# One factor for two query blocks in a differential attention on one Trainium2 core

## The chip, the core and the metric

The kernel runs on one core of a Trainium2 chip. A core has five engines with a queue each: TensorE (PE, matmuls and transposes, into PSUM), VectorE (DVE), ScalarE (ACT, exponentials and copies), GpSimd (POOL) and SyncE (SP, which here issues the DMAs). An engine takes its instructions strictly in the order of its queue; between engines, semaphores hold an instruction back until what it reads is there and what it overwrites has been read. The metric is the device time of one execution in microseconds (us). Before the change the median of three executions is 1089.66 us (1088.95 to 1091.61).

## The reference

One layer of a hybrid decoder, sequence 1024, width 1024, all in float32: a norm, one input projection, four mixers side by side (pooling, short convolution, a Conformer convolution, differential attention), an output projection, and a gated feed-forward part of width 2816. The change is in the attention: 4 heads, each with two softmaxes over 32-wide queries and keys, values 64 wide.

```python
def block(args):                      # 8 query blocks of 128 rows
    qblk, start = args
    ...
    sc = jnp.einsum('bqhmd,bkhmd->bhmqk', qblk, k).astype(jnp.float32) * scale + bias
    sc = jnp.where(dist >= 0, sc, NEG_INF)
    p = jax.nn.softmax(sc, axis=-1)
    a = p[:, :, 0] - lam * p[:, :, 1]
    return jnp.einsum('bhqk,bkhd->bqhd', a.astype(v.dtype), v)
...
o = rms_norm(o, subln_g) * (1.0 - lam_init)
```

## The kernel before

The program has three parts: norm and input projection with the convolutions (to about 255 us), attention with the output projection filled in between (about 255 to 430 us), and the feed-forward part. A float32 matmul is made of three matmuls of high and low parts (lines 138 to 140, and 599 to 601 for the filler).

Attention works in 16 units: `for u in range(16)` with p = 0 to 3 (a pair of query blocks, i = 0 and 1, so that keys up to w = 128 x (2p + 1 + i) count) and head h = 0 to 3 inside. In a unit, for each block i and for each softmax m = 1, then 0:

- line 668: TensorE makes the scores `sc` (queries QT by keys KT). For p = 0 and 1 both softmaxes of a block share one PSUM tile (`both`), for p = 2 and 3 each has its own; there are two such tiles in turn.
- lines 675 and 676: VectorE takes the minimum over the columns (`fmx`, then `mx` with the bias table `tb` added in place; the scores are negated). 675 is there from p = 1 on.
- line 679: ScalarE writes the exponentials `pt` and their row sums into `lt`. The tile `pt` of m = 1 has two buffers (PT1), that of m = 0 has four (PT0).
- lines 681 to 683: VectorE makes the factor `cf` = l0 * (-lam) / l1, in a reciprocal and a one-column multiplication, and combines `pt0 + cf * pt1` in place. The row is not divided by l0; the norm behind it makes up for this.

Then, for each pair of key blocks: line 694 transposes the combined tile on TensorE (`tp`), line 698 copies it on ScalarE and line 699 subtracts on VectorE for the low part (`at`), and line 703 multiplies by the values (`av`). Every second head ends with a transposition of the output (715), every fourth with its norm (725 to 734). `prep_q` (lines 500 to 508) prepares the queries of the next pair in between.

What sets the order: each engine's queue is made when the program is built, by a scheduler that goes by the order of the code as priority and by its own model of times and buffers. The filler matmuls of the output projection are handed out by a fixed list of counts (FQ) at marked places, each behind a given TensorE instruction. So where an instruction stands in a queue does not change at run time. DMAs are issued by SyncE; none belongs to the lines of the change.

Of the kernel before, what the change touches and what calls it, by code (L numbers as in the profile page):

```python
# [11 lines left out]
F = mybir.dt.float32  # L12
R = mybir.dt.float32r
AF = mybir.ActivationFunctionType
ALU = mybir.AluOpType
# [4 lines left out]
P = 128  # L20
# [46 lines left out]
def tile_hybrid(ctx, tc, x, norm1_g, w_in, pool_w, pool_scale, sconv_w, conf_w, conf_b, ln_g, ln_b,  # L67
# [3 lines left out]
    V, A, G, T = nc.vector, nc.scalar, nc.gpsimd, nc.tensor  # L71
# [11 lines left out]
    def pool(name, bufs=1, side="left", **kw):  # L83
        return tc.tile_pool(name=name, bufs=bufs, side=side, reuse_waits="tile", **kw)
# [4 lines left out]
    sm = ctx.enter_context(pool("sm"))  # L89
# [28 lines left out]
    def cp(e, dst, src):  # L118
        if e == 0:
            A.copy(dst, src)  # L120
        else:
            (V, G)[e - 1].tensor_copy(dst, src)
# [119 lines left out]
    for p in range(4):  # L242
# [13 lines left out]
        h = p // 2  # L256
# [80 lines left out]
    nlam = const.tile([P, 1], F, name="nlam")  # L337
# [242 lines left out]
    def ps_sc():  # L580
        return pss.tile([P, 1024], F, name="sc", tag="sc")

    def ps_tp():
        return psp.tile([P, 512], F, name="tp", tag="tp")

    def ps_av():
        return psq.tile([P, 512], F, name="av", tag="av")
# [48 lines left out]
    def fill1(ins, n=None):  # L636
        for _ in range(next(slots, 0) if n is None else n):
            while fillq:
                f = next(fillq[0], None)
                if f is not None:  # L640
                    if GATE:
                        with tc.issue_after(ins.ins):
                            f()
                    else:
                        f()
                    break
                fillq.pop(0)
# [4 lines left out]
    def unit(u, p, h):  # L652
        if h == 0:
            pend["lt"] = sm.tile([P, 4, 2, 2], F, name="lt", tag="lt", bufs=2)
            pend["o"] = sm.tile([P, 2, 4, 64], F, name="o", tag="kn")
        lt, o = pend["lt"], pend["o"]
        Ps = []
        for i in range(2):
            w = P * (2 * p + 1 + i)
            nw = min(w, 256)  # L660
            pts = [None, None]
            both = ps_sc() if p < 2 else None
            for m in MO:
                hm = 2 * h + m
                sc = ps_sc() if both is None else both[:, 512 * m:512 * m + 512]
                for c0 in range(0, w, 512):
                    n = min(max(w - c0, 256), 512)
                    ins = T.matmul(sc[:, c0:c0 + n], lhsT=QT[p, h // 2][:, hm % 4, i * P:(i + 1) * P],
                                   rhs=KT[h // 2][:, hm % 4, c0:c0 + n], start=True, stop=True)
                fill1(ins)  # L670
                mx = sm.tile([P, 1], F, name="mx", tag="mx", bufs=4)
                init = 3.0e38
                if w > 256:
                    init = sm.tile([P, 1], F, name="fmx", tag="fmx", bufs=2)
                    V.tensor_reduce(init, sc[:, 0:w - 256], axis=AX.X, op=ALU.min)
                V.tensor_tensor_reduce(out=sc[:, w - nw:w], in0=sc[:, w - nw:w], in1=tb[:, h, 256 - nw:], scale=1.0,  # L676
                                       scalar=init, op0=ALU.add, op1=ALU.min, accum_out=mx)
                pts[m] = ap4.tile([P, S], F, name="pt", tag=f"pt{m}", bufs=PT1 if m else PT0)
                A.activation(pts[m][:, 0:w], sc[:, 0:w], AF.Exp, bias=mx, scale=-1.0, accum_out=lt[:, h, m, i:i + 1])  # L679
            cf = sm.tile([P, 1], F, name="cf", tag="cf", bufs=4)  # L680
            V.reciprocal(cf, lt[:, h, 1, i:i + 1])
            V.scalar_tensor_tensor(cf, lt[:, h, 0, i:i + 1], nlam, cf, op0=ALU.mult, op1=ALU.mult)
            V.scalar_tensor_tensor(pts[0][:, 0:w], pts[1][:, 0:w], cf, pts[0][:, 0:w], op0=ALU.mult, op1=ALU.add)  # L683
            Ps.append(pts[0])
        if h % 2 == 0:
            pend["av"] = ps_av()
        avs = pend["av"]
        av = avs[:, (h % 2) * 256:(h % 2) * 256 + 256]
        for kb in range(p + 1):
            ps = ps_tp()  # L690
            blocks = [(a, i) for a in range(2) for i in range(2) if 2 * kb + a <= 2 * p + i]
            nb = len(blocks) * P
            for j, (a, i) in enumerate(blocks):
                ins = T.transpose(ps[:, j * P:(j + 1) * P], Ps[i][:, (2 * kb + a) * P:(2 * kb + a + 1) * P], ident)
            marks.append(ins)
            fill1(ins)
            at = ap4.tile([P, 2, 512], R, name="at", tag="at", bufs=ATB)
            A.copy(at[:, 0, 0:nb], ps[:, 0:nb])
            V.tensor_tensor(at[:, 1, 0:nb], ps[:, 0:nb], at[:, 0, 0:nb].bitcast(F), op=ALU.subtract)
            for s in range(2):  # L700
                for a in range(2):
                    n = min(nb - 256 * a, 256)
                    ins = T.matmul(av[:, 256 - n:256], lhsT=VV[kb][:, a, h, :], rhs=at[:, s, 256 * a:256 * a + n],
                                   start=(kb == 0 and a == 0 and s == 0), stop=(kb == p and a == 1 and s == 1))
                if s == 0:
                    fill1(ins)
        marks.append(ins)
        fill1(ins)
        if h % 2 == 1:
            oT = sm.tile([P, 512], F, name="oT", tag="sq")  # L710
            cp(OTE[u // 2], oT, avs)
            ps = ps_tp()
            for hh in range(2):
                for i in range(2):
                    ins = T.transpose(ps[:, (i * 2 + hh) * P:(i * 2 + hh + 1) * P], oT[:, hh * 256 + i * P:hh * 256 + (i + 1) * P], ident)
            marks.append(ins)
            fill1(ins)
            psv = ps.rearrange("p (i h d) -> p i h d", i=2, h=2)
            ov = o[:, :, h - 1:h + 1, :]
            cp(OVE[u // 2], ov, psv[:, :, :, 64:128])  # L720
            V.tensor_tensor(ov, ov, psv[:, :, :, 0:64], op=ALU.add)
        if h == 3:
            of = o.rearrange("p i h d -> p (i h) d")
            osq = sm.tile([P, 8, 64], F, name="osq", tag="sq")
            A.activation(osq, of, AF.Square)
            rr = sm.tile([P, 2, 4], F, name="rr", tag="rr", bufs=2)
            rrf = rr.rearrange("p i h -> p (i h)")
            V.tensor_reduce(rrf, osq, axis=AX.X, op=ALU.add)
            l0 = lt[:, :, 0, :]
            l2 = sm.tile([P, 4, 2], F, name="l2", tag="l2", bufs=2)  # L730
            V.scalar_tensor_tensor(l2, l0, EPS, l0, op0=ALU.mult, op1=ALU.mult)
            V.scalar_tensor_tensor(rr, rr, 1.0 / 64, l2.rearrange("p h i -> p i h"), op0=ALU.mult, op1=ALU.add)
            G.tensor_tensor(rrf, rrf, mhalf[:, 0:8], op=ALU.pow)
            (G if X5[PO.index(p)] else V).tensor_tensor(qn[p].rearrange("p i (h d) -> p (i h) d", h=4), of, rrf.unsqueeze(2).broadcast_to([P, 8, 64]),
                            op=ALU.mult)
# [85 lines left out]
    for u in range(16):  # L821
        j, h = u // 4, u % 4
        p = PO[j]
        if h == 0 and j > 0:
            fillq.append(out_attn(PO[j - 1]))
            if j == 3:
                fillq.append(norm2(PO[0]))
                fillq.append(norm2(PO[1]))
        if h == PQ1 and j > 0:
            prep_q(p, 1, ps_tp, 4, fill1)  # L830
        if h == PQ0 and j < 3:
            prep_q(PO[j + 1], 0, ps_tp, 4, fill1)
        unit(u, p, h)
# [345 lines left out]
```

## Time and profile before

| | |
|---|---|
| median of 3 executions | 1089.66 us |
| the profiled execution | 1092.04 us |
| its span, first to last instruction | 1090.2 us |
| TensorE clock, mean granted | 0.995 |
| PE / DVE / ACT / POOL busy | 97 / 67 / 40 / 21% |

A busy share is over the whole span. In a window of time the busy times of the engines can be set against the length of the window; what is missing is idle time of that engine. Matmuls overlap each other, so that a busy TensorE is not one at its peak.

### The profile page before, as it was taken

What the parts mean: (1) busy time and instruction counts of PE and PEld (TensorE: products, weight loads), DVE (VectorE), ACT (ScalarE), POOL (GpSimd) and SP (SyncE); (2) the same over time, 40 slices, a digit from 0 to 9 for tenths busy, and PEclk for the clock granted to TensorE, in tenths of its full rate; (3) what the DMA queues carried; (4) which work ended last, traced back from release to release, by engine and by line L of the source; (5) the groups of instructions that cost most, each with busy time, mean ns of one, the idle gap of its engine ahead of it and who ended that gap; (6) DMA issues with size and microseconds to landing.
All of it is one profiled execution on the core that took longest, in us unless ns stands there. A gap on an engine that the chain in (4) does not pass through costs nothing.

```text
span 1090.2 us, 13509 instructions
## 1 busy us (share of the span) xinstructions
PE 1054.3 (97%) x5203; PEld 875.9 (80%) x5203; DVE 734.6 (67%) x1127; ACT 439.4 (40%) x710; POOL 224.1 (21%) x202
## 2 busy tenths in 40 slices
PE   7989999998989999999999999999999999999998
PEld 6858888997778876787778888888888888888886
DVE  5599965556899977788677766565556666655541
ACT  5511123544787676442333332333333244333320
POOL 5224423673757743210000000000000000000000
PEclk9989999999999999999999999999999999999999
DMA  8230111110111122013567663233223268766731
GB/s 217 45 97 25 54 39 39 40 40 30 39 50 58 40 78 58 1 58 135 201 238 267 240 242 111 73 126 108 86 97 126 72 237 295 264 193 199 234 108 39
DMA packets 89664, 128.04 MB, mean 117 GB/s; under 512 B 17112, under 2 KB 57600, under 8 KB 87040
## 3 DMA queue, kind: packets, MB, share of 16 engines
q1 hardware_dynamic: 89600, 127.18, 35.6%
q8 instruction: 41, 0.67, 0.2%
q14 instruction: 23, 0.19, 0.1%
HBM read 94.13 MB, written 33.04 MB: 117 GB/s over the span
## 4 chain that ended last, share of the span: by engine, by line
PE 78%; DVE 11%; DMA 6%; ACT 2%; issue 1%; POOL 1%; SPq 0%; ACTq 0%; POOLq 0%; DVEq 0%
PE sb L140 10%; PE sb L138 10%; PE sb L139 10%; PE mm L139 6%; PE mm L140 6%; PE mm L138 6%; PE dx L140 3%; PE dx L139 3%; PE dx L138 3%; PE dy L140 3%; PE dy L139 2%; PE dy L138 2%; DMA wd<-in_w_down_dram 2%; DMA dT<-wd 2%; DVE pt L683 1%
## 5 line engine op out<-in xcount | busy, mean ns | idle before, releaser
L138 PE MATMUL sb<-T,rhi 128*128 128x512 f32 x320 | 125.6, 393 | 0.0
L140 PE MATMUL sb<-T,rlo 128*128 128x512 f32 x320 | 125.4, 392 | 0.0
L139 PE MATMUL sb<-T,rhi 128*128 128x512 f32 x320 | 125.4, 392 | 0.0
L906 DVE TENSOR_TENSOR dq<-ds,dq 128x2048 fp32r<-128x2048 f32 x35 | 80.1, 2290 | 60.4 <-ACT dq L905 60.4
L905 ACT CAST dq<-ds 128x2048 fp32r<-128x2048 f32 x35 | 66.8, 1911 | 105.5 <-PE dy L140 40.4
L134 POOL TENSOR_TENSOR wlo<-st,whi 128x1024 fp32r<-128x1024 f32 (+2 forms) x30 | 73.3, 2447 | 111.4 <-ACT whi L120 98.1
L139 PE MATMUL mm<-hT,whi 128*128 128x512 f32 (+1 forms) x224 | 82.1, 371 | 1.0 <-DVE hT L200 1.0
L138 PE MATMUL mm<-hT,whi 128*128 128x512 f32 (+1 forms) x224 | 80.3, 374 | 1.8 <-ACT hT L199 1.8
L140 PE MATMUL mm<-hT,wlo 128*128 128x512 f32 (+1 forms) x224 | 81.5, 368 | 0.0
L312 DVE SCALAR_TENSOR_TENSOR t<-u,cw,t 128x1023 f32<-128x1023 f32 (+28 forms) x58 | 71.2, 1265 | 0.7
L138 PEld LDWEIGHTS sb<-T,rhi 128*128 128x128 f32 x320 | 60.1, 188 | 13.8 <-DVE afs L1014 0.3
L139 PEld LDWEIGHTS sb<-T,rhi 128*128 128x128 f32 x320 | 60.1, 188 | 13.5
L140 PEld LDWEIGHTS sb<-T,rlo 128*128 128x128 f32 x320 | 60.0, 188 | 13.5
L905 ACT CAST rhi<-st 128x1024 fp32r<-128x1024 f32 x28 | 29.4, 1052 | 84.6 <-PE sb L139 53.0
L140 PE MATMUL dx<-dq 128*128 128x512 f32 x160 | 62.3, 390 | 0.0
L139 PE MATMUL dx<-dq 128*128 128x512 f32 x160 | 62.2, 389 | 0.0
L138 PE MATMUL dx<-dq 128*128 128x512 f32 x160 | 61.8, 389 | 0.0
L679 ACT ACTIVATE pt<-sc,mx 128x128 f32<-128x128 f32 (+7 forms) x64 | 47.6, 747 | 18.7 <-DVE mx L676 18.6
L138 PE MATMUL mm<-whi,hT 128*128 128x256 f32 x192 | 54.8, 289 | 0.0
L139 PE MATMUL mm<-wlo,hT 128*128 128x256 f32 x192 | 54.5, 285 | 0.0
L140 PE MATMUL mm<-whi,hT 128*128 128x256 f32 x192 | 54.4, 284 | 0.0
L120 ACT CAST whi<-st 128x1024 fp32r<-128x1024 f32 x28 | 29.4, 1050 | 59.7 <-PE mm L139 53.0
(342 smaller groups left out, 2690.1 us busy)
## 6 DMA issues: line engine op xcount, KB each, us to landing
ds<-dL SPq DMA_DIRECT2D x35, 512.0 KB, 4.1
wd<-in_w_down_dram SPq DMA_DIRECT2D x10, 1024.0 KB, 5.1
dT<-wd SPq DMA_DIRECT2D x10, 1024.0 KB, 4.0
dL<-afs SPq DMA_DIRECT2D x10, 1024.0 KB, 4.1
ds<-dT SPq DMA_DIRECT2D x20, 512.0 KB, 5.3
st<-in_w_in_dram SPq DMA_DIRECT2D x18, 512.0 KB, 3.8
st<-in_w_gate_dram SPq DMA_DIRECT2D x15, 512.0 KB, 4.3
st<-in_w_up_dram SPq DMA_DIRECT2D x15, 512.0 KB, 3.7
```

The source lines that it names most:

```text
L120: A.copy(dst, src)
L134: G.tensor_tensor(lo[:, nv:], st[:, nv:], hi[:, nv:].bitcast(F), op=ALU.subtract)
L138: T.matmul(ps, lhsT=L[0], rhs=Rr[0], start=first, stop=False, skip_group_check=more)
L139: T.matmul(ps, lhsT=L[0], rhs=Rr[1], start=False, stop=False, skip_group_check=more)
L140: return T.matmul(ps, lhsT=L[1], rhs=Rr[0], start=False, stop=last, skip_group_check=more)
L312: V.scalar_tensor_tensor((z if s == 30 else acc)[:, s:], u[:, :S - s], w[:, 30 - s:31 - s], acc[:, s:], op0=ALU.mult, op1=ALU.add)
L679: A.activation(pts[m][:, 0:w], sc[:, 0:w], AF.Exp, bias=mx, scale=-1.0, accum_out=lt[:, h, m, i:i + 1])
L683: V.scalar_tensor_tensor(pts[0][:, 0:w], pts[1][:, 0:w], cf, pts[0][:, 0:w], op0=ALU.mult, op1=ALU.add)
L905: A.copy(hi, src)
L906: (eng or V).tensor_tensor(lo, src, hi.bitcast(F), op=ALU.subtract)
```

## The change

The factor is made once in a unit, for both query blocks, as two columns: one reciprocal and one multiplication. Both combinations stand behind it, so behind the exponentials of both blocks. In the changed file the lines behind line 683 are three further down: the combination is 686, the transposes 697, the subtraction 702.

```diff
-            cf = sm.tile([P, 1], F, name="cf", tag="cf", bufs=4)
-            V.reciprocal(cf, lt[:, h, 1, i:i + 1])
-            V.scalar_tensor_tensor(cf, lt[:, h, 0, i:i + 1], nlam, cf, op0=ALU.mult, op1=ALU.mult)
-            V.scalar_tensor_tensor(pts[0][:, 0:w], pts[1][:, 0:w], cf, pts[0][:, 0:w], op0=ALU.mult, op1=ALU.add)
-            Ps.append(pts[0])
+            Ps.append(pts)
+        cf = sm.tile([P, 2], F, name="cf", tag="cf", bufs=4)
+        V.reciprocal(cf, lt[:, h, 1, :])
+        V.scalar_tensor_tensor(cf, lt[:, h, 0, :], nlam, cf, op0=ALU.mult, op1=ALU.mult)
+        for i, (a, b) in enumerate(Ps):
+            w = P * (2 * p + 1 + i)
+            V.scalar_tensor_tensor(a[:, 0:w], b[:, 0:w], cf[:, i:i + 1], a[:, 0:w], op0=ALU.mult, op1=ALU.add)
+        Ps = [a for a, b in Ps]
```

The scheduler orders the engines anew from the first unit to the end of attention; SyncE's queue stays as it was, and so does everything behind attention.

VectorE from the end of unit 6 into unit 7 (p = 1). Before; `pt_3047` is the combined block 1 of unit 6, `sc_3079` and `sc_3099` are the scores of unit 7:

```order
L683 SCALAR_TENSOR_TENSOR pt_3047<-pt_3040,cf_3049,pt_3047 128x512
L721 TENSOR_TENSOR o_2779<-o_2779,tp_2969 128x2x128
L681 RECIPROCAL cf_3095<-lt_2778 128x1
L675 TENSOR_REDUCE fmx_3090<-sc_3079 128x1
L675 TENSOR_REDUCE fmx_3107<-sc_3099 128x1
L676 ISA sc_3079,mx_3089<-sc_3079,tb_783,fmx_3090 128x256
L676 ISA mx_3089 128x1
L676 ISA sc_3099,mx_3106<-sc_3099,tb_783,fmx_3107 128x256
L676 ISA mx_3106 128x1
L682 SCALAR_TENSOR_TENSOR cf_3095<-lt_2778,nlam_627,cf_3095 128x1
```

Now; `pt_3009` and `pt_3025` are the two blocks of unit 6, `sc_3058` and `sc_3074` the scores of unit 7:

```order
L683 SCALAR_TENSOR_TENSOR cf_3027<-lt_2766,nlam_627,cf_3027 128x2
L686 SCALAR_TENSOR_TENSOR pt_3009<-pt_2993,cf_3027,pt_3009 128x384
L686 SCALAR_TENSOR_TENSOR pt_3025<-pt_3018,cf_3027,pt_3025 128x512
L702 TENSOR_TENSOR at_3040<-tp_3033,at_3040 128x512
L675 TENSOR_REDUCE fmx_3069<-sc_3058 128x1
L675 TENSOR_REDUCE fmx_3082<-sc_3074 128x1
L702 TENSOR_TENSOR at_3051<-tp_3047,at_3051 128x384
L676 ISA sc_3058,mx_3068<-sc_3058,tb_783,fmx_3069 128x256
L676 ISA mx_3068 128x1
L676 ISA sc_3074,mx_3081<-sc_3074,tb_783,fmx_3082 128x256
```

The subtraction for unit 6's own transposes has come to stand ahead of the minima of unit 7.

TensorE at the same place. Before; `sc_3079` is the m = 0 score of unit 7, block 0, and `tp_3054` holds transposes of unit 6:

```order
L668 MATMUL sc_3099<-KT1_1365,QT_2750 128x512
L668 MATMUL sc_3079<-KT1_1365,QT_2750 128x384
L505 MATMUL tp_2997<-ident_89,kst_2994 128x128 x4
L600 MATMUL fm_2909<-wlo_2430,sp_2986 128x512
L601 MATMUL fm_2909<-whi_2429,sp_2986 128x512
L694 MATMUL tp_3054<-ident_89,pt_3027 128x128
L694 MATMUL tp_3054<-ident_89,pt_3047 128x128
```

Now; `sc_3058` is the m = 0 score of unit 7, block 0, and `tp_3033` and `tp_3047` hold transposes of unit 6:

```order
L697 MATMUL tp_3033<-ident_89,pt_3009 128x128
L697 MATMUL tp_3047<-ident_89,pt_3009 128x128
L697 MATMUL tp_3033<-ident_89,pt_3025 128x128
L697 MATMUL tp_3033<-ident_89,pt_3009 128x128
L697 MATMUL tp_3033<-ident_89,pt_3025 128x128
L601 MATMUL fm_3000<-whi_2417,sp_3001 128x512
L599 MATMUL fm_3000<-whi_2417,sp_3001 128x512
L697 MATMUL tp_3047<-ident_89,pt_3025 128x128 x2
L600 MATMUL fm_3000<-wlo_2418,sp_3001 128x512
L668 MATMUL sc_3058<-KT1_1365,QT_2738 128x384
```

The m = 0 score of unit 7 stood ahead of unit 6's transposes and now stands behind them.

VectorE late in unit 13 (p = 3). Before; `cf_3986` is the factor of block 1 and `sc_3977` its last scores, `sc_4070` belongs to unit 14:

```order
L676 ISA sc_3977,mx_3980<-sc_3977,tb_783,fmx_3981 128x256
L676 ISA mx_3980 128x1
L675 TENSOR_REDUCE fmx_4074<-sc_4070 128x1
L699 TENSOR_TENSOR at_3886<-tp_3879,at_3886 128x512
L676 ISA sc_4070,mx_4073<-sc_4070,tb_783,fmx_4074 128x256
L676 ISA mx_4073 128x1
L682 SCALAR_TENSOR_TENSOR cf_3986<-lt_3809,nlam_627,cf_3986 128x1
L699 TENSOR_TENSOR at_3906<-tp_3899,at_3906 128x512
L683 SCALAR_TENSOR_TENSOR pt_3984<-pt_3975,cf_3986,pt_3984 128x1024
```

Now; `cf_3943` is the one factor of unit 13, `sc_3934` the last scores, `sc_4028` belongs to unit 14:

```order
L676 ISA sc_3934,mx_3937<-sc_3934,tb_783,fmx_3938 128x256
L676 ISA mx_3937 128x1
L676 ISA sc_4028,mx_4031<-sc_4028,tb_783,fmx_4032 128x256
L676 ISA mx_4031 128x1
L702 TENSOR_TENSOR at_3867<-tp_3860,at_3867 128x512
L683 SCALAR_TENSOR_TENSOR cf_3943<-lt_3773,nlam_627,cf_3943 128x2
L686 SCALAR_TENSOR_TENSOR pt_3923<-pt_3913,cf_3943,pt_3923 128x896
L686 SCALAR_TENSOR_TENSOR pt_3941<-pt_3932,cf_3943,pt_3941 128x1024
```

Between the last minimum and the factor that needs its exponential there stand two steps now and three before, and both combinations follow.

## Rows read from the trace of the kernel before

**Rows 1.** The page, busy time, share of the span and instructions of each engine.

```profile
PE 1054.3 (97%) x5203; PEld 875.9 (80%) x5203; DVE 734.6 (67%) x1127; ACT 439.4 (40%) x710; POOL 224.1 (21%) x202
```

**Rows 2.** Stretches: length, busy PE, PEld, DVE, ACT, POOL; clock, DMA share, GB/s.

```profile
255.00:310.00 55.00, 50.27 (x264) 39.76 (x263) 47.13 (x158) 37.07 (x110) 34.66 (x40) 0.97 0.12 37
310.00:331.00 21.00, 18.35 (x109) 15.19 (x108) 20.39 (x51) 16.62 (x37) 15.10 (x13) 1.00 0.23 78
331.00:400.00 69.00, 65.95 (x379) 56.01 (x378) 64.48 (x140) 49.76 (x99) 43.98 (x43) 1.00 0.17 55
...
262.00:266.00 4.00, 3.95 (x14) 3.20 (x15) 2.62 (x11) 2.38 (x9) 0.08 (x1) 0.57 0.04 10
```

**Rows 3.** Chain that ended last, around 300 and 375 us: start, us, what.

```profile
299.92 0.53 DVE fmx L675 x2
300.45 0.40 DVE sc L676
...
302.01 0.75 DVE pt L683
...
375.20 1.47 DVE pt L683
```

**Rows 4.** Timeline, VectorE, second combinations: start, us, engine, line, operation.

```profile
262.28 0.48 DVE L683 SCALAR_TENSOR_TENSOR pt<-pt,cf 128x256 f32<-128x256 f32 x1
...
277.92 0.49 DVE L683 SCALAR_TENSOR_TENSOR pt<-pt,cf 128x256 f32<-128x256 f32 x1
...
294.94 0.83 DVE L683 SCALAR_TENSOR_TENSOR pt<-pt,cf 128x512 f32<-128x512 f32 x1
...
309.29 0.75 DVE L683 SCALAR_TENSOR_TENSOR pt<-pt,cf 128x512 f32<-128x512 f32 x1
...
318.01 1.02 DVE L683 SCALAR_TENSOR_TENSOR pt<-pt,cf 128x768 f32<-128x768 f32 x1
...
396.95 2.28 DVE L683 SCALAR_TENSOR_TENSOR pt<-pt,cf 128x1024 f32<-128x1024 f32 x1
```

**Rows 5.** Groups by line in attention: count, busy us, mean ns, idle before, releaser.

```profile
L682 DVE SCALAR_TENSOR_TENSOR cf<-lt,nlam,cf 128x1 f32<-128x1 f32 x32 | 12.7, 396 | 4.7 <-ACT pt L679 4.3
L681 DVE RECIPROCAL cf<-lt 128x1 f32<-128x1 f32 x32 | 4.9, 153 | 0.4 <-ACT pt L679 0.3
L699 DVE TENSOR_TENSOR at<-tp,at 128x512 fp32r<-128x512 f32 (+1 forms) x35 | 21.6, 628 | 0.7 <-ACT at L698 0.7
...
L698 ACT CAST at<-tp 128x512 fp32r<-128x512 f32 x24 | 14.0, 592 | 5.3 <-PE tp L694 5.3
L679 ACT ACTIVATE pt<-sc,mx 128x256 f32<-128x256 f32 x8 | 3.8, 477 | 3.7 <-DVE mx L676 3.7
```

**Rows 6.** Timeline, units 5 and 6 on VectorE, ScalarE and TensorE.

```profile
291.05 0.62 DVE L683 SCALAR_TENSOR_TENSOR pt<-pt,cf 128x384 f32<-128x384 f32 x1
...
294.03 0.57 ACT L679 ACTIVATE pt<-sc,mx 128x384 f32<-128x384 f32 x1
...
296.47 0.97 ACT L698 CAST at<-tp 128x512 fp32r<-128x512 f32 x2 [0.79 <-PE tp L694]
...
298.89 0.44 PE L668 MATMUL sc<-KT,QT 128*128 128x512 f32 x1
...
300.94 0.69 ACT L679 ACTIVATE pt<-sc,mx 128x512 f32<-128x512 f32 x1 [0.81 <-DVE mx L676]
...
301.76 0.22 DVE L682 SCALAR_TENSOR_TENSOR cf<-lt,nlam,cf 128x1 f32<-128x1 f32 x1 [0.44 <-ACT pt L679]
```

**Rows 7.** Timeline, the last factor on VectorE and GpSimd beside it.

```profile
394.50 2.40 POOL L134 TENSOR_TENSOR wlo<-st,whi 128x1024 fp32r<-128x1024 f32 x1 [0.73 <-ACT whi L120]
...
396.05 0.87 DVE L682 SCALAR_TENSOR_TENSOR cf<-lt,nlam,cf 128x1 f32<-128x1 f32 x1 [0.42 <-ACT pt L679]
```

**Rows 8.** Timeline, TensorE, first transposes of units 8 and 15.

```profile
321.05 0.60 PE L694 MATMUL tp<-ident,pt 128*128 128x128 f32 x4
...
402.34 0.62 PE L694 MATMUL tp<-ident,pt 128*128 128x128 f32 x4
```

## The prediction

> **What bounds the kernel now.** I read the totals of the page first, then a table of stretches, then the chain of waits, then the instructions of one pair of units in order of time. The page has TensorE busy for 97% of the span [rows 1]: most of the kernel is a queue of matmuls with nothing between them, and a change elsewhere counts only where TensorE stands. The table shows the only part that this change touches, attention, from 255 to 400 us [rows 2]. From 255 to 310 us TensorE is idle for 55.0 - 50.3 = 4.7 us, from 310 to 331 for 2.7, from 331 to 400 for 3.0. VectorE is the fullest of the helpers: 47.1 of 55.0, 20.4 of 21.0, 64.5 of 69.0. One more thing is in the first stretch: from 262 to 266 us the granted clock is 0.57, near the lower of the two levels (1.2 of 2.4 GHz), and 1.00 from 310 us on.
>
> The chain of waits says who paces attention: around 300 us and again from 371 us it runs from one VectorE step straight to the next [rows 3]. So VectorE time there is real time, but only until TensorE's own queue is the later of the two.
>
> I number the units 0 to 15 in program order: four heads at each p = 0 to 3, two query blocks i = 0, 1 in each, two softmaxes m = 1, 0 in each block. A unit is done when the second combination (L683, i = 1) ends. Those ends [rows 4]: unit 0 at 262.76 us, 3 at 278.41, 5 at 295.77, 7 at 310.04, 8 at 319.03, 15 at 399.23. Unit 6 ended at 302.76 (the 302.01 step of [rows 3]).
>
> **What goes.** 32 reciprocals become 16 and 32 factor steps become 16; each keeps its fixed time, since it had one column and now has two. A reciprocal is 0.153 us, a factor step 0.396 in the mean [rows 5], but the bare one is 0.22 (unit 6, 301.76 us [rows 6]). The rest of the mean is a wait: the last factor step began at 396.05 us and ended at 396.92, and the GpSimd subtraction beside it ran from 394.50 to 396.90 [rows 7]. Does that wait go with the instruction? I take it that it does not, because the combination, which has the same kind of operands, stands right behind and meets the same GpSimd step. So 16 x (0.153 + 0.22) = 6.0 us of VectorE time go; with the waits 16 x (0.153 + 0.396) = 8.8.
> The Trainium skill, page "SBUF — State Buffer", section "Who interferes with whom", says that a VectorE instruction with two SBUF inputs and a GpSimd instruction that reads SBUF exclude each other for the whole instruction, whoever starts first. The rows of 394.50 and 396.05 us agree to 0.02 us. By that rule the wait only moves to the next two-input step, which is the 6.0 us; if it went away with the step it would be 8.8.
> The same skill, page "Perfetto Trace Analysis", section "Optimizing Scalar/DVE Operations", says that grouping operations helps a saturated engine, and that where an engine is not saturated but causes bubbles elsewhere, breaking them up lets work end sooner. VectorE has 7.9 us idle before 310 us and 0.6 in the 21 us behind it [rows 2], so by that rule the change helps late and hurts early, which is how the sum below comes out.
>
> **What is moved.** The combination of i = 0 used to stand before the second block's work was through; now both stand behind the fourth exponential. In the pair of units that I follow, block 0 of unit 5 was combined at 291.05 us and block 1 at 294.94, so block 0 becomes about 3.9 us later relative to its unit. Who waits for it? The transposes of a unit need both blocks in nearly all units, so they lose nothing. But there are only two buffers for the m = 1 exponentials, and each is free only when its combination has read it. The next unit's first exponential (294.03 us, unit 6) could start before unit 5 was complete. Now it cannot start before unit 5's block 0 is combined, which is where unit 5 ends. Behind this exponential, at p = 0 and 1, queues the m = 0 score matmul (it goes into the same PSUM tile), behind that its minimum, behind that the rest of the unit. The order of TensorE shows it: the m = 0 scores of unit 7 stood ahead of unit 6's transposes and now stand behind them. On VectorE the subtraction at<-tp, which waits for transposes and copy, now stands ahead of the next unit's minima.
>
> **A unit at p = 1 after the change**, from the end of one second combination (0) to the next: the copy of the transposes starts 0.70 later (295.77 to 296.47 [rows 6]), takes 0.59 [rows 5]: 1.3. The subtraction 0.6: 1.9. Two reductions 0.53 (299.92 us [rows 3]): 2.4. Another subtraction, the smaller one, 0.55: 3.0. Two minima at 0.40 (300.45): 3.8. The exponential of block 1, from its start to the next step that may use it, 0.82 (300.94 to 301.76): 4.6. Its scores 0.44 (298.89): 5.0. Reductions and minima 1.33: 6.4. Exponential 0.82: 7.2. Factor 0.25. Combinations 0.62 and 0.75: 8.8. Before, unit 5 to 6 took 7.0 and 6 to 7 took 7.3, so 1.8 + 1.5 = 3.3 are lost. Unit 4 to 5 has other VectorE work (the norm's steps) in the 1.3 us in which it would stand: nothing lost.
> **At p = 0** the same chain with exponentials of 256 columns (0.48 [rows 5]) comes to 0.7 + 0.5 + 0.5 + 0.7 + 0.6 + 0.3 + 0.8 + 0.6 + 0.25 + 0.83 = 5.8, the other steps estimated from those of p = 1 by their width. Bounds: 5.8, and 6.8 where TensorE's filler matmuls stand between the two scores. I take 6.3. Before, three units took 278.41 - 262.76 = 15.65, so 5.2 each: 3 x 1.1 = 3.3 lost. Unit 0 itself has nothing ahead of it and gains one factor and one reciprocal: -0.4. Unit 3 to 4 was paced by TensorE and has room: -0.7.
> Sum up to unit 8: 3.3 + 3.3 - 0.4 - 0.7 = 5.5 us late on VectorE. TensorE takes unit 8's transposes at 321.05, 2.0 after they are ready [rows 8], so TensorE is 3.5 late.
>
> **What is given back at p = 2 and 3.** There the two score tiles in turn take the place of the shared tile, and VectorE has a full queue. It saves 8 x (0.153 + 0.22) = 3.0. It gains waits: in the order, between the last minimum of a unit and its factor stand mostly 0.5 to 1.0 us of steps, and the exponential takes 0.82 at 512 columns and more at 1024, so some 0.4 in each unit: 3.2, less what it waited there before (0.42 in the last unit [rows 7]): 2.8. Net -0.2. Its idle time from 310 to 400 us was 0.6 + 4.5 = 5.1 [rows 2], of which I let two thirds be used up: 3.4. So VectorE ends some 5.5 - 0.2 - 3.4 = 1.9 late. Unit 15's transposes were taken 3.1 us after they were ready (399.23, 402.34), so VectorE's lateness is covered. TensorE's own 3.5 shrink by its idle time from 310 to 400, at most 2.7 + 3.0 = 5.7; I take 2.2 of it, since the two engines are seldom idle for the same reason. That leaves +1.3 us. Behind attention the program is the same.
>
> **The number.** The profiled execution took 1092.04 us, its span 1090.2 with 1.8 around it; it lies 2.4 above the median of the three timed, 1089.66. The sum is a difference, so I put it on the median: 1091.0. About 0.3%, 3.3 us, is what a measurement of this kernel tells from no change.
>
> **Rivals.**
> Slower: nothing is given back. The price is the 5.5 us of the two buffers, 1095.2; if the low clock of 262 to 266 us comes a second time (half speed for 4 us, 1.7 us) 1096.9. It decides from the point at which TensorE stands over 7 us in all for the transposes up to unit 8. For it: TensorE's idle time behind 331 us is small (3.0 of 69 us), and lateness on a full queue stays. Against it: the idle time of both engines from 310 to 400 us.
> Faster: the chain of the two buffers hides behind TensorE's filler, and VectorE's 6.0 us reach the end wherever VectorE paces, which by the chain is about three quarters of the units: 4.5 us, 1085.2. For it: [rows 3]. Against it: before, a unit at p = 1 took 7.0, under the 8.8 of the chain.
> The forecast, within 3.3 us of before: loss early, most of it given back.
> Chances: forecast 0.49, slower 0.33, faster 0.18. The range reaches down to the faster case and up to the slower one with a second spell of the low clock: 1085.5 to 1097.
>
> **What would show it.** Right: second combinations of units 6 and 7 some 8.8 us apart, the m = 1 exponential of each next unit starting just behind a combination, TensorE waiting for L686 by several microseconds up to 318 us, and VectorE's span from unit 8 to 15 shorter than 80.2 us. Wrong: units 5 to 7 no further apart than 7.3 us (then it is faster), or TensorE's idle time at p = 2 and 3 as large as before (then it is slower).

## The result and the profile after

The changed kernel takes 1119.49 us in the median (1118.47 to 1121.27), beside 1089.93 for the kernel before on the same chip: a ratio of 1.027, 95% interval 1.0252 to 1.0284, or 29.5 us more. 1091.0 was predicted, in a range up to 1097.0.

The page of the changed kernel, busy time and instructions of each engine:

```profile
PE 1067.4 (96%) x5203; PEld 881.6 (79%) x5203; DVE 729.9 (65%) x1095; ACT 441.6 (40%) x710; POOL 221.6 (20%) x202
```

VectorE has 32 instructions and 4.7 us less than in [rows 1]. TensorE has the same 5203 instructions and takes 13.1 us longer over them; the other half of the longer span is idle time. The next table shows where. First the stretches of [rows 2] in the changed kernel, then one stretch from 255 us to 640 us before the end, first of the changed kernel (221.7 us), and in the fence behind it of the kernel before (195.2 us):

```profile
255.00:310.00 55.00, 47.53 (x227) 35.50 (x225) 36.42 (x118) 31.06 (x91) 31.27 (x36) 0.94 0.10 34
310.00:331.00 21.00, 16.23 (x70) 12.12 (x70) 12.98 (x37) 12.16 (x30) 7.08 (x8) 0.84 0.06 17
331.00:400.00 69.00, 60.94 (x318) 50.72 (x317) 51.60 (x117) 43.24 (x91) 43.12 (x44) 0.93 0.16 53
...
255.00:476.70 221.70, 194.46 (x976) 152.62 (x974) 155.09 (x366) 133.08 (x294) 108.61 (x107) 0.95 0.14 43
```

```profile
255.00:450.20 195.20, 181.13 (x982) 147.26 (x980) 162.09 (x401) 131.59 (x295) 110.62 (x107) 0.99 0.16 49
```

By the choice of its ends, what lies ahead of this stretch and behind it is as long in both kernels, so the whole difference of the spans, 26.5 us, lies in it. TensorE's idle time in it is 27.2 us beside 14.1 (+13.2), its busy time 194.5 beside 181.1 (+13.3), and its mean clock 0.95 beside 0.99. VectorE, which had 20.4 of 21 us filled from 310 to 331, now has 13.0: it has become the engine that waits.

For what? The two factor groups of the changed kernel, 255 to 431 us (count, busy us, mean ns, idle time just before them and its releaser):

```profile
L683 DVE SCALAR_TENSOR_TENSOR cf<-lt,nlam,cf 128x2 f32<-128x2 f32 x16 | 5.7, 357 | 8.4 <-ACT pt L679 8.4
L682 DVE RECIPROCAL cf<-lt 128x2 f32<-128x2 f32 x16 | 2.6, 163 | 10.8 <-ACT pt L679 10.8
```

VectorE stood 19.2 us ahead of these two groups, for exponentials; before it was 5.1 [rows 5]. The steps themselves take 8.3 us in place of 17.6. And in the order of time, VectorE's combinations of units 3, 4 and 5, each with the first exponential of the next unit on ScalarE:

```profile
282.14 1.17 DVE L686 SCALAR_TENSOR_TENSOR pt<-pt,cf 128x128 f32<-128x128 f32 x2
...
283.02 0.58 ACT L679 ACTIVATE pt<-sc,mx 128x384 f32<-128x384 f32 x1 [1.50 <-DVE pt L686]
...
290.55 1.76 DVE L686 SCALAR_TENSOR_TENSOR pt<-pt,cf 128x384 f32<-128x384 f32 x2
...
291.26 0.58 ACT L679 ACTIVATE pt<-sc,mx 128x384 f32<-128x384 f32 x1
...
299.61 1.86 DVE L686 SCALAR_TENSOR_TENSOR pt<-pt,cf 128x384 f32<-128x384 f32 x2
...
300.76 0.58 ACT L679 ACTIVATE pt<-sc,mx 128x384 f32<-128x384 f32 x1
```

A row with x2 holds both combinations of a unit. Each next unit's first exponential begins inside it, when block 0 has been combined. Before, the exponential of unit 6 began 0.9 us before block 1 of unit 5 was combined (294.03 and 294.94 [rows 6, 4]); block 0's combination had begun 3.0 us earlier, at 291.05. From 255 us to the end of attention ScalarE waits for combinations as follows (us in total, times, longest); the kernel before has no such wait:

```profile
ACT pt L679 <- DVE pt L686: 7.6, 8, 2.1
```

What TensorE waited for, from 255 us to the end of attention, in the changed kernel and then before (us in total, times, longest):

```profile
PE sc L668 <- ACT pt L679: 10.4, 11, 2.3
PE tp L505 <- POOL kst L501: 5.1, 3, 4.2
PE tp L697 <- DVE pt L686: 4.1, 7, 1.4
PE av L706 <- DVE at L702: 2.5, 5, 1.2
```

```profile
PE av L703 <- DVE at L699: 3.0, 3, 1.3
PE tp L505 <- POOL kst L501: 2.6, 3, 1.1
PE tp L694 <- DVE pt L683: 1.9, 4, 0.8
PE sc L668 <- ACT pt L679: 1.5, 2, 0.8
```

The largest is new: score matmuls that wait for an exponential to give up their PSUM tile. So a late buffer reaches TensorE more by the exponential and the score tile than by the transposes.

The ends of the second combinations, worked out from the rows of L683 before and L686 after, show how the lateness runs:

| unit | 0 | 3 | 5 | 7 | 8 | 9 | 11 | 13 | 15 |
|---|---|---|---|---|---|---|---|---|---|
| before, us | 262.8 | 278.4 | 295.8 | 310.0 | 319.0 | 330.0 | 350.0 | 376.7 | 399.2 |
| after, us | 261.0 | 283.3 | 301.5 | 322.3 | 333.6 | 349.6 | 374.5 | 402.7 | 429.5 |
| later by | -1.7 | 4.9 | 5.7 | 12.2 | 14.6 | 19.6 | 24.5 | 26.0 | 30.2 |

(The end of unit 0 differs by up to 2.6 us between traces with the same queues; it is 260.2 us in the run pad below. So a single entry is no better than that; the growth along the row is.) Nothing is given back at p = 2 and 3; as much again is added. (Of the 30.2 us, 26.5 are left at the end of the program, since more of the filler has been done by the end of attention: 2208 matmuls of the profile began before 429.5 us, 2195 before 399.2 in the kernel before.) Part of the lateness is the clock. Stretches of 4 us of the changed kernel (length, busy PE, PEld, DVE, ACT, POOL, then the granted clock):

```profile
316.00:320.00 4.00, 1.56 (x5) 0.78 (x5) 2.60 (x11) 1.42 (x5) 0.30 (x1) 0.92 0.05 20
320.00:324.00 4.00, 3.25 (x11) 2.38 (x12) 2.85 (x10) 2.27 (x6) 0.00 (x0) 0.50 0.00 0
324.00:328.00 4.00, 4.00 (x16) 3.26 (x15) 1.38 (x3) 2.00 (x6) 0.74 (x1) 0.73 0.03 6
332.00:336.00 4.00, 1.12 (x8) 0.76 (x6) 4.00 (x11) 2.52 (x5) 1.81 (x1) 1.00 0.06 23
336.00:340.00 4.00, 2.72 (x11) 2.53 (x12) 1.86 (x5) 2.38 (x6) 3.82 (x4) 0.55 0.35 131
340.00:344.00 4.00, 4.00 (x16) 3.42 (x15) 2.81 (x7) 2.35 (x5) 2.96 (x3) 0.59 0.00 0
360.00:364.00 4.00, 1.87 (x10) 1.24 (x9) 4.00 (x9) 1.82 (x5) 0.00 (x0) 0.97 0.00 0
364.00:368.00 4.00, 4.00 (x17) 3.39 (x16) 0.74 (x5) 3.81 (x10) 2.38 (x3) 0.61 0.00 0
```

Three times TensorE was busy for 1.1 to 1.9 of 4 us, and each time the next 4 to 8 us ran at 0.50 to 0.73, near the lower level (1.2 of 2.4 GHz). 4 us times what is missing from 1.00, over these eight rows, is 8.5 us of full speed; counted only for the time in which TensorE was busy, 7.3. The first and the third of these stretches lack work mostly because TensorE waits for score tiles. The second doesn't:

```profile
337.28 1.11 PE L505 MATMUL tp<-ident,kst 128*128 128x128 f32 x4 [4.15 <-POOL kst L501]
```

TensorE stood 4.15 us for a step of `prep_q` on GpSimd. In GpSimd's queue that step (336.50 us) now stands behind a subtraction of 2.35 us for the weights of the filler (334.19 us); before it stood ahead of it (319.77 and 320.72 us). This comes from the new order of a queue and not from a late buffer. In the kernel before there is no low clock behind 310 us [rows 2].

### The profile page after: what moved, and what is told of

Same layout as the page of the kernel before. It is cut to its first block, busy times and chain, and to the rows that moved or that the text cites. A ratio compares the mean times of both kernels' runs of the same rounds, so it can differ in the third digit from the quotient of the medians.

```text
span 1116.7 us, 13503 instructions
## 1 busy us (share of the span) xinstructions
PE 1067.4 (96%) x5203; PEld 881.6 (79%) x5203; DVE 729.9 (65%) x1095; ACT 441.6 (40%) x710; POOL 221.6 (20%) x202
## 4 chain that ended last, share of the span: by engine, by line
PE 73%; DVE 10%; DMA 8%; ACT 3%; issue 3%; POOL 2%; SPq 1%; ACTq 0%; POOLq 0%; DVEq 0%
PE sb L138 9%; PE sb L140 9%; PE sb L139 9%; PE mm L139 6%; PE mm L140 6%; PE mm L138 6%; PE dx L140 3%; PE dx L139 3%; PE dx L138 3%; DMA wd<-in_w_down_dram 3%; DMA dT<-wd 3%; PE dy L140 2%; PE dy L139 2%; PE dy L138 2%; DVE pt L686 2%
## 5 line engine op out<-in xcount | busy, mean ns | idle before, releaser
L908 ACT CAST rhi<-st 128x1024 fp32r<-128x1024 f32 x28 | 29.4, 1049 | 84.9 <-PE sb L139 44.3
```

The costliest lines, as they stand in the source:

```text
L908: A.copy(hi, src)
```

## The experiments

Ratios are to the kernel before, timed on the same chip beside the run, with 95% intervals. The first four separate buffers, place in the code, and VectorE time.

**after_b4**: the changed kernel with four buffers for the exponentials of m = 1.

```diff
-pts[m] = ap4.tile([P, S], F, name="pt", tag=f"pt{m}", bufs=PT1 if m else PT0)
+p1p = mid.enter_context(pool("p1p", 2))
...
+pts[m] = p1p.tile([P, S], F, name="pt", tag="pt") if m and i else ap4.tile([P, S], F, name="pt", tag=f"pt{m}", bufs=PT1 if m else PT0)
```

> The changed kernel, but the m = 1 exponentials of block 1 have two buffers of their own, so four in all. Theory A (with two buffers a unit's first exponential waits for the combination of the unit before, and from there the whole unit): the loss goes, 1085 to 1093 us, and no ScalarE exponential waits for a combination. Theory B (what costs is the place of the combinations in the fixed queues: with both late, the transposes have no work to hide behind): 1110 us or more. Theory C (a two-column factor step is dear): 1115 to 1120.

Measured 1102.41 us, 1.012 (1.009 to 1.0149), in the range of none of the three. No exponential waits for a combination any more, as A has it. 17 of the 29.5 us go with the buffers, and most of the low clock with them: its mean over the span is 0.995, as before (0.985 in the changed kernel). 12.4 us stay. The scheduler knows the number of buffers: with four, the queues of all four engines come out in another order than in the changed kernel. The 17 us are the price of two buffers with the order made for them; the wait by itself is not separated from the order.

**before_b4**: the same edit in the kernel before.

> The kernel before with the same four buffers. Theory A: block 0's buffer was free early anyway, so 1087 to 1091 us. If more buffers alone let the scores run further ahead, 1080 to 1086, and the gain in the other run must be read against this one. Theory B and C: as before, 1090.

Measured 1090.05 us, 1.0003 (0.9987 to 1.0019). All queues are those of the kernel before. That kernel does not lack buffers; the change made them scarce.

**move_only**: the lines behind the loop over the blocks as in the change, but a reciprocal and a factor of their own for each block.

```diff
+        for i, (a, b) in enumerate(Ps):
+            cf = sm.tile([P, 1], F, name="cf", tag="cf", bufs=4)
+            V.reciprocal(cf, lt[:, h, 1, i:i + 1])
...
```

> Both combinations behind the exponentials of both blocks, but each block with its own reciprocal and factor step, two buffers. Theories A and B: the move is the loss, so 1117 to 1126 us, the changed kernel plus up to 6 us of VectorE steps. Theory C: near before, 1088 to 1093.

Measured 1090.0 us, 1.0004 (0.9987 to 1.0021). The experiment didn't do what it was meant to: with nothing that ties block 0's combination to block 1, the scheduler made the queues of the kernel before again, instruction for instruction on all four engines. So the place in the code costs nothing; the shared factor does, since it makes block 0's combination depend on block 1's exponentials.

**extra**: the kernel before with a second, unused reciprocal and factor in each block.

> The kernel before with a second reciprocal and a second factor step for each block, whose result nobody reads: 32 x (0.153 + 0.22) = 11.9 us more on VectorE. If VectorE's queue paces attention: 1098 to 1102 us. If its time is mostly covered, as the forecast's idle times say: 1091 to 1095. Half of the difference to before is what the merging can be worth at most.

Measured 1105.86 us, 1.0149 (1.012 to 1.0179). That is 15.9 us for the 11.9 expected; the run pad below takes 5 of it away, so about 11. In the trace the added steps are busy for 15.1 us, but VectorE's total rises by 7.5 only (742.1 beside 734.6), since other steps get shorter. So VectorE time added here costs something near its length; the price of one us is not better known than that.

The next four ask where in attention the loss arises, and whether the dependency alone makes it.

**late**: one reciprocal for both blocks, but a factor step for each.

```diff
+        cr = sm.tile([P, 2], F, name="cr", tag="cr", bufs=4)
+        V.reciprocal(cr, lt[:, h, 1, :])
+        for i, (a, b) in enumerate(Ps):
+            cf = sm.tile([P, 1], F, name="cf", tag="cf", bufs=4)
+            V.scalar_tensor_tensor(cf, lt[:, h, 0, i:i + 1], nlam, cr[:, i:i + 1], op0=ALU.mult, op1=ALU.mult)
...
```

> Leaves the arithmetic whole. One reciprocal for both blocks as in the changed kernel, but the factor step done once per block (16 more factor steps than the changed kernel, 16 x 0.153 = 2.4 us of VectorE, at the 1.3 us per us that the run with the extra steps showed about 3 us). Both combinations still have to stand behind the exponentials of both blocks. Theory A (the late combination of block 0 costs the time, through the buffers and the VectorE queue): 1117 to 1124 us. Rival B (the two-column factor step itself, or its reading of two columns, is what costs): back near 1090 us.

Measured 1108.26 us, 1.0168 (1.0139 to 1.0196), between the two. My description of it was wrong in one point: here block 0's combination depends only on the m = 1 exponentials of both blocks, and in the queue it went ahead of block 1's m = 0 part. That is part of the delay and part of the loss: 18.8 us, of which some 5 are those of the run pad below.

**new_p01** and **new_p23**: the changed form at p = 0 and 1 only, and at p = 2 and 3 only.

> The changed form only in query pairs p=0 and p=1 (units 0 to 7), the old form in p=2 and p=3. Theory A (attention is paced by VectorE to its end, so lateness stays): the second combination of unit 7 ends about 12 us later than before and that lateness is still there at the end, 1099 to 1104 us. Rival B (p=2 and p=3 give lateness back, as the prediction had it, as long as they are in the old form): 1090 to 1093 us. Rival C (the stretch of low granted clock at 315 to 355 us is started by the waits of p=1 and costs most of the rest): the low stretch appears here too and the time is 1108 us or more.

> The changed form only in p=2 and p=3 (units 8 to 15). Theory A (each unit in the changed form loses by itself): units 8 to 15 lose about the 18 us that they lost in the changed kernel, 1105 to 1110 us. Rival C (their loss in the changed kernel came with the low clock that p=1 started): under 8 us, 1090 to 1098 us. Prediction's step (units of p=2 and p=3 stand still less for the new form than they gain): 1087 to 1091 us.

Measured 1116.23 us, 1.0245 (1.0224 to 1.0266), and 1106.88, 1.0158 (1.0135 to 1.0181). The two losses add to more than the whole, which is what led to the run pad.

**pool_cf**: the kernel before with reciprocal and factor on GpSimd (a power of -1, then a product).

> The kernel before with the reciprocal and the factor step of all 32 blocks on GpSimd (a power of -1 and a product with two factors) in place of VectorE: VectorE has 32 x (0.153 + 0.22) = 11.9 us less in its queue, but each combination waits some 0.8 us more for its factor (GpSimd's power on few columns took 0.70 us in the trace). If VectorE's queue is worth over 1 us per us, as the run with the extra steps showed, and the wait is covered by other VectorE work: 1078 to 1085 us. If the wait is not covered (VectorE stands behind it in order): 32 x 0.8 = 26 us longer less 12 to 16, so 1095 to 1105 us.

Measured 1105.91 us, 1.0151 (1.0129 to 1.0173). VectorE has 9.8 us less to do (724.8 us), but in attention it stood 15.0 us for the factor: a helper that takes work off a queue and answers late cost more than the work. (It adds a small constant tile and has 437 matmuls in the stretch that the run pad below looks at, so a little of it may be that.)

**pad**: the kernel before with four more small tiles of 4 bytes per partition, one of them written once. **pad2**: the same with 64 bytes.

```diff
+            if p == 0 and h == 0 and i == 0:
+                jk = sm.tile([P, 1], F, name="jk", tag="jk", bufs=4)      # pad2: [P, 16]
+                G.memset(jk, 0.0)
```

> The kernel before with one more name for small tiles (four tiles of 4 bytes per partition, one of them written once), as the runs late, extra, new_p01 and new_p23 had. These four had 433 matmuls per 100 us in stretches where TensorE was never idle 300 us before the end, and before, after and the four-buffer kernels 439. Theory A (the shifted place of the tiles behind it makes those matmuls slower): 1092 to 1094 us and 433 matmuls. Rival B (something else of those kernels): 1089 to 1091 us and 439.

> As pad, with the four unused small tiles 64 bytes per partition each in place of 4, so that everything behind them lies 16 times as far from its place in the kernel before. If what costs the 5 us in pad is where the tiles behind start, not how many names there are, the number of matmuls per 100 us differs from pad's 433 (439 in the kernel before): 1089 to 1092 us if it is back at 439. If any shift costs: 1094 to 1097 us and 433.

Measured 1095.34 us, 1.004 (1.0025 to 1.0055), and 1089.89, 0.9998 (0.9985 to 1.0011). In pad, the queues of TensorE, VectorE and ScalarE are instruction for instruction those of the kernel before. Its attention ends 2.2 us earlier (397.0, 399.2), yet behind it pad takes 697.1 us and the kernel before 691.0. The same 100 us of pad and of the kernel before, TensorE never idle:

```profile
690.20:790.20 100.00, 100.00 (x433) 81.31 (x432) 58.29 (x79) 32.57 (x45) 0.00 (x0) 1.00 0.27 90
```

```profile
690.20:790.20 100.00, 100.00 (x439) 82.05 (x439) 59.29 (x79) 33.70 (x47) 0.00 (x0) 1.00 0.29 98
```

Six matmuls fewer in 100 us at a granted clock of 1.00. late, extra, new_p01 and new_p23 each added a name for a small tile and have 433 too, so some 5 us of each are not their edit (p01c and p23c below, with the queues of the last two and 439 matmuls, are 4.1 and 4.2 us shorter).

**p01c** and **p23c**: new_p01 and new_p23 with one name for all factor tiles; the queues of TensorE and VectorE are the same.

> new_p01 again (changed form in p=0 and p=1 only, two buffers), with one name for the small factor tiles as in the changed kernel; the order of the instructions on every engine is that of new_p01. Theory A (the run pad showed that one more name for small tiles costs 5 us by itself, so new_p01 carried these): 1109 to 1113 us and 439 matmuls per 100 us in the stretch 400 to 300 us before the end. Rival B (the whole of new_p01's 26.5 us is the change): 1114 to 1118 us.

> new_p23 again (changed form in p=2 and p=3 only, two buffers), with one name for the small factor tiles. Theory A (in p=2 and p=3 the cost is the combination of block 0 behind the last exponential, the same with two buffers as with four, and new_p23 carried 5 us of the tiles' place): 1100 to 1104 us, as the changed kernel with four buffers (1102.4). Rival B (two buffers cost more there too): 1105 to 1109 us.

Measured 1112.17 us, 1.0208 (1.0191 to 1.0224), and 1102.64, 1.0111 (1.0095 to 1.0127), both with 439 matmuls: 21.8 and 12.3 us. Together that is 34.1; the whole change costs 29.5. Two things follow. At p = 2 and 3 the loss doesn't need the buffers: with four of them in after_b4 it is as large in total (12.4 us). That they cost nothing there isn't shown, since in p23c ScalarE still waits for combinations (2.6 us in 3 waits) and the clock falls below 0.7 in three stretches of 4 us behind 310 us, in after_b4 in none. And what p = 0 and 1 cost doesn't stay there: in p01c unit 7 is 10.6 us late and unit 15, eight units of the old form later, 21.4. Of these further 10.8 us the rows below (310 to 350 us of p01c, clock 0.92 and 0.82) show at most 21 x 0.08 + 19 x 0.18 = 5.1 of lost full speed (4.2 for the time in which TensorE was busy):

```profile
310.00:331.00 21.00, 16.67 (x81) 12.74 (x81) 15.17 (x41) 11.56 (x28) 7.52 (x8) 0.92 0.12 39
331.00:350.00 19.00, 15.67 (x78) 13.31 (x78) 15.88 (x41) 15.18 (x33) 14.80 (x11) 0.82 0.24 82
```

The cause of the other 6 or so stays open. One candidate is the order: the code of units 8 to 15 is the old one in p01c, but the scheduler ordered them anew. Of the 186 VectorE instructions behind unit 7 at most 128 are still in the order of the kernel before.

**b4_p01** and **b4_p0**: four buffers, and the changed form at p = 0 and 1, or at p = 0 alone.

> The changed form in p=0 and p=1 only, with four buffers for the m=1 exponentials. In the run of the whole changed kernel with four buffers the second combination of unit 7 ended only 0.8 us later than before, and units 8 to 15 lost 10.4 us. Theory A (in p=0 and p=1 only the wait for a buffer costs; with buffers the changed form is free there): 1088 to 1092 us. Rival B (a loss of p=0 and p=1 grows in whatever follows, as the +11.6 us at unit 7 became +26 us in the run with the changed form in p<2): 1096 us or more.

> A version that could beat both: four buffers and the changed form in p=0 only. In the run with four buffers and the changed form in p=0 and p=1, units 0 to 3 gained 1.9 us on the kernel before (counted from the run pad, whose attention starts level with it) and units 4 to 7 lost 4. If that gain stays: 1087.5 to 1089 us. Rival (it is taken back behind unit 3, as TensorE has the same work to do): 1089.5 to 1091 us.

Measured 1091.91 us, 1.0007 (0.9994 to 1.0019), and 1089.21, 0.9994 (0.9985 to 1.0003). With buffers the changed form costs nothing measurable at p = 0 and 1, and the clock stays at 1.00 from 310 to 400 us. In b4_p01 the queues behind unit 7 are again those of the kernel before (all 186 VectorE instructions in their order), so it shows what becomes of a lateness there: beside before_b4 and counted from unit 0, unit 7 is 2.8 us late and unit 15 2.3. The changed form doesn't pay either: no version here is measurably faster than the kernel before.

**skip_b4** and **skip_before**: after_b4 and before_b4, and at p = 2 and 3 the combination of block 0 left out.

```diff
+            if p < 2 or i == 1:
                 V.scalar_tensor_tensor(a[:, 0:w], b[:, 0:w], cf[:, i:i + 1], a[:, 0:w], op0=ALU.mult, op1=ALU.add)
```

> The changed kernel with four buffers, and in p=2 and p=3 the combination of block 0 left out (8 instructions of 0.93 to 1.9 us; block 0's second softmax is not added there). Theory A (the 12 us that four buffers leave come from block 0's combination standing behind the last exponential, ahead of the transposes): they go with it, and this kernel and the kernel before with the same left out end within 3 us of one another. Rival B (they come from the shared factor step or from the order of the queues): it stays 8 to 12 us behind that other kernel.

> The kernel before with four buffers, and in p=2 and p=3 the combination of block 0 left out, as the one beside it. If VectorE's queue paces p=2 and p=3 here, 8 x 1.2 = 9.6 us less of it give 5 to 10 us: 1080 to 1085 us. If block 0's combination lies beside the exponentials of block 1 and costs nothing: 1088 to 1091 us.

Measured 1094.95 us, 1.0041 (1.0025 to 1.0056), and 1091.8, 1.0013 (0.9998 to 1.0028). The distance of the two kernels shrinks from 12.4 us to 3.1. Before the change, this combination is worth nothing: eight of them less gain no time. After it, they cost some 7 to 9 us. The ends of the second combinations say where the 3.1 us are: skip_b4 is 4.0 us behind skip_before at unit 7 already (311.99 and 308.03) and 5.1 at unit 15 (403.35 and 398.24), so units 8 to 15 lose 1.1 us in this pair; with the combination they lose 10.3 (after_b4 beside before_b4: 2.1 at unit 7, 12.4 at unit 15). The transposes didn't go ahead instead: those of a unit still begin behind its second combination, but for one matmul each in two of the eight. What block 0's combination stands behind is seen at unit 15. after_b4, ScalarE's last exponential, then VectorE:

```profile
405.56 1.12 ACT L680 ACTIVATE pt<-sc,mx 128x1024 f32<-128x1024 f32 x1
406.56 0.20 ACT L680 ACTIVATION_READ_ACCUMULATOR pt<-sc,mx 128x1 f32 x1
406.80 0.22 DVE L684 SCALAR_TENSOR_TENSOR cf<-lt,nlam,cf 128x2 f32<-128x2 f32 x1 [0.16 <-ACT pt L680]
407.05 3.38 DVE L687 SCALAR_TENSOR_TENSOR pt<-pt,cf 128x896 f32<-128x896 f32 x2
```

and before_b4:

```profile
389.80 1.15 DVE L684 SCALAR_TENSOR_TENSOR pt<-pt,cf 128x896 f32<-128x896 f32 x1
...
393.63 1.12 ACT L680 ACTIVATE pt<-sc,mx 128x1024 f32<-128x1024 f32 x1
394.64 0.20 ACT L680 ACTIVATION_READ_ACCUMULATOR pt<-sc,mx 128x1 f32 x1
394.87 0.86 DVE L683 SCALAR_TENSOR_TENSOR cf<-lt,nlam,cf 128x1 f32<-128x1 f32 x1 [0.42 <-ACT pt L680]
395.77 2.29 DVE L684 SCALAR_TENSOR_TENSOR pt<-pt,cf 128x1024 f32<-128x1024 f32 x1
```

Block 0 was combined (389.80) while the exponentials of block 1 were still to come. Now it stands between the last exponential and the transposes. Over units 8 to 15, the time from the end of the last exponential (its row sum read) to that of the second combination is 19.7 us before, 19.8 in before_b4 and 29.2 in after_b4: 9.5 us more, beside the 10.3 that these units lose there. Block 0's combinations take 9.1 us in it.

## Why the prediction was wrong

**What goes**: 6.0 us of VectorE time were expected and 4.7 are gone from its total. The steps that were merged take 9.3 us less (17.6 to 8.3); the rest has come back in other steps of VectorE. But the saving was worth nothing that shows: with four buffers the changed form at p = 0, or at p = 0 and 1, gains no measurable time (b4_p0, b4_p01), and in skip_before eight combinations taken away gain none either. The chain of waits [rows 3] showed VectorE on the path before the change; it does not show what comes next when a step is taken off that path.

**What is moved**: right in kind, too small in size. The exponential of the next unit does start just behind a combination, and units at p = 1 are 9.0, 9.2, 11.6 and 9.2 us apart (8.8 predicted for the last two), those at p = 0 6.6, 8.5 and 7.2 (6.3). At unit 8 VectorE is 14.6 us late, not 5.5. Counted from unit 0, p = 0 lost 6.7 us (3.3 predicted), the last two steps of p = 1 6.5 (3.3), the step from unit 4 to 5 1.0 (nothing), and the step from unit 7 to 8 2.4, which the sum didn't have. The chain had the second score of a pair behind the exponential that holds its tile, as a term of VectorE's time. What it left out is that TensorE stands still meanwhile, with the filler and the transposes in line behind (10.4 us in 11 waits, 7.2 up to unit 8), and that the clock then falls. The wait named as a sign, TensorE for L686, is 2.7 us up to 318 us and 4.1 in all; the one that I hadn't named is the larger.

"The transposes of a unit need both blocks in nearly all units, so they lose nothing" is a step that failed. They need both, and therefore wait for all that stands behind the last exponential: one combination before, two now. That is most of the 12 us of p = 2 and 3, where I had a net of -0.2.

**What is given back at p = 2 and 3**: this step failed too, and with it the sum. From unit 8 to 15 the lateness doubled, 14.6 to 30.2 us, instead of shrinking. I took idle time (5.1 us of VectorE, 5.7 of TensorE) for room in which lateness is made good. A good part of it was time in which one waited for the other: before, from 310 to 400 us, TensorE stood 3.0 us for VectorE's subtractions and VectorE 2.0 for TensorE's scores. b4_p01, with the old queues at p = 2 and 3, gave back 0.5 of 2.8 us. One of the prediction's own signs of being wrong came: between the ends of units 7 and 15 TensorE is idle for 12.2 us, before for 5.0. And VectorE takes 95.8 us from unit 8 to 15, not under 80.2.

The Trainium skill, page "Perfetto Trace Analysis", section "Optimizing Scalar/DVE Operations", says of grouping that it can improve throughput if the engine is saturated. From this the prediction drew that the change helps late. By busy time VectorE was nearly full from 310 to 400 us (84.9 of 90 us [rows 2]), and grouping there cost 12.3 us (p23c). The measurement decides: here a nearly full engine whose results are waited for in turn was helped by an early result more than by fewer instructions.

**The rivals**: the slower one had the right sign and part of the mechanism (two buffers, nothing given back, the low clock), with a price of 5.5 us and one spell of the low clock at 1.7. There were three, of 7.3 to 8.5 us together. It named TensorE's standing for the transposes over 7 us up to unit 8 as the point from which it decides; there were 2.7. What reached 7 us there was the wait for score tiles.

In sums, by the runs: two buffers and the order of the queues that the scheduler makes for them 17 us (after against after_b4, the clock spells among them), block 0's combination behind the last exponential most of the other 12.4 (9.3 of it gone in the pair with that combination left out). How the 17 us divide between the wait for a buffer, the order and the clock stays open, as do some 6 us in p01c.

## What to carry to other kernels

When two steps are merged, the merged one takes the latest of both sets of inputs: list all that was done early and is now behind the last input, and charge it in full to whoever needs the result, before counting the instructions saved. Idle time of an engine in a chain that passes between engines is not slack; ask what it waits for before booking lateness against it. Where a buffer is held longer, follow it on through the engine that fills it to the tile that this engine empties. Where a scheduler orders the queues, compare the queues of two kernels before a loss is put down to one wait: here even units whose code had not changed got another order (p01c).

## What was not expected of the hardware

Four more tiles of 4 bytes per partition slow matmuls by 1.4% (433 in place of 439 in 100 us) for some 300 us far behind them, at a granted clock of 1.00 and with the same queues; with 64 bytes nothing is lost. Experiments that add a small tile carry about 5 us of this in this kernel, so a control run with an unused one is worth its price. That it is the place of the tiles behind them is likely and not shown: no run shows an address, and the factor tiles of the changed kernel, also four, are 4 bytes larger each and cost no matmul (439).

The clock fell after stretches of 4 us in which TensorE was busy for 1.1 to 1.9, and stood at 0.50 to 0.73 for the next 4 to 8 us. TensorE lacked 2.4, 2.9 and 2.1 us of work in these three stretches, and the spells lost 2.8, 2.9 and 1.6 us of full speed in the time in which it was busy: by this estimate a wait can cost itself again. The estimate is not a measured price. In the four executions of p23c the mean clock lay between 0.985 and 0.994, which is 10 us of full speed over the span, and the times lay only 2.1 us apart.
